# Sixty places in a hand-ordered prologue: an RWKV time-mix kernel with the steps of pairs 4 to 13 moved past their neighbours

## The chip, the core and the metric

The kernel runs on one core of a Trainium2 chip. The core has five engines that work side by side, each with its own queue of instructions: PE (TensorE, matrix products), DVE (VectorE), ACT (ScalarE), POOL (GpSimd) and SP (SyncE, which here only issues transfers). Sixteen DMA engines move data between the chip's main memory and the core's memory. The metric is the device time of one execution in microseconds; lower is better. The kernel before took 287.9 us, the median of three runs (287.43 to 288.99).

## What is computed

For each of 16 batches and 256 channels, a recurrence runs over 2048 time steps. It keeps a weighted sum `aa` of the values v, a sum of weights `bb`, and a running exponent `pp` that keeps the exponentials in range:

```python
for t in range(seq_len):
    kk = k[b, t, :].copy()
    vv = v[b, t, :].copy()
    ww = u + kk
    qq = np.maximum(pp, ww)
    e1 = np.exp(pp - qq)
    e2 = np.exp(ww - qq)
    output[b, t, :] = (e1 * aa + e2 * vv) / (e1 * bb + e2 + 1e-08)
    ww = pp - w + kk
    qq = np.maximum(ww, kk)
    e1 = np.exp(ww - qq)
    e2 = np.exp(kk - qq)
    aa = e1 * aa + e2 * vv
    bb = e1 * bb + e2
    pp = qq
```

k, v and the output are 33.5 MB each in fp32, so 67 MB are read and 33.5 MB written.

## The kernel before

Time is cut into 16 chunks of 128 steps. For one chunk, the 16 batches are handled four at a time; such a quarter of a chunk is called a pair here (pair n = 4 * chunk + quarter, n from 0 to 63), and the four pairs of one chunk are a group. One pair is a tile of 128 time steps by 4 batches by 256 channels, 512 KB of k and 512 KB of v.

The work on a pair is split into named steps, each on one engine. In the order of the data:

- LK n and LV n load k and v. The first three pairs are loaded by SP, the others by POOL, in one queue. k of pairs 3 to 11 is loaded straight into a `kr` buffer (four of them); from pair 12 on it goes into a `kf` buffer (five), and RK n rounds it into `kr`, on DVE or, for one pair in four, on POOL. Pairs 0 to 2 also have an RK. v goes into a `vr` buffer (four).
- R q n and L q n (q = 0 or 1, `rows` and `logs`) are PE's work that builds the exponents of pair n in one of two PSUM buffers, X0 or X1. X q n (`exps`) is ACT's exponential of it into the ring `EZR`, and frees the X buffer and, with q = 1, the PE side of `kr`.
- CV n casts v to bf16 into `vb` (two buffers; DVE for the first ten pairs, POOL after that), TV n (DVE) multiplies, and S n (PE) sums over time into `TOT`.
- Once per group c, after the fourth S: CS c (DVE copies TOT), TU c (PE turns it), SL c (ACT, logarithm), FR c and OF c (DVE), SW c (ACT), CH c and SS c (DVE), TK c (PE turns the states back into `TURN`), BK c (DVE copies TURN to `cb`), and SN c and KP c (DVE, what the next group starts from).
- DEN n and NUM n (PE) form denominator and numerator; DEN uses an X buffer, NUM the buffer `num`. LN n and INV n (ACT) form the inverse, MUL n (DVE) multiplies into `ot`, and ST n (SP) stores it, ten pairs behind the load.

Between PE's steps stand "zeros", products of a zero tile written to `TURN`, whose result nobody uses. `Z`, `Z0` and `ZAT` say how many stand ahead of which kind of step; none are written in the stretch of the plan that lies from a TK to its BK (the flag `quiet`).

The order of everything is set by a planner at the end of the function. Each step has a place, a number; places come from the table `P`, and an entry of `AT` replaces the place of one step by name ("TK 0": 7.205). The planner takes again and again the first step in order of place whose inputs have been planned and whose buffer is free:

```python
todo = sorted(ops, key=lambda x: ops[x]["place"])
while todo:
    for name in todo:
        o = ops[name]
        if all(x not in ops or "done" in ops[x] for x in o["after"]) and (xs if o["take"] == "X" else free.get(o["take"], 1)):
            break
```

An engine runs its steps in just this order, and waits at the head of its queue. Which X buffer an R, L, X or DEN gets follows from the order too: the buffer that was freed first in the plan. A kr slot that a load takes must have been read by the L that used it; the waits for that are worked out from the order as well.

Of the kernel before, what the change touches and what calls it, by code (L numbers as in the profile page):

```python
# [15 lines left out]
def kernel(  # L16
# [46 lines left out]
         "Z": {"DEN": 0, "L": 1, "NUM": 0, "TK": 4, "S": 0, "TU": 1, "R": 0}}  # L63

    AT = {"INV 55": 69.0, "SL 15": 69.1, "LN 56": 69.2, "SW 15": 75.7, "FR 15": 69.3, "TU 0": 5.01, "FR 0": 5.02,
# [4 lines left out]

    ZAT = {"DEN 0": 4, "TU 1": 4, "R 0 11": 4}

# [123 lines left out]
    X = [psx.tile([128, 2, D], F32, tag=f"X{a}", name=f"X{a}") for a in range(2)]  # L196
# [31 lines left out]
    AS, D1, L1, A0, FR, BC, A2 = range(7)  # L228
# [268 lines left out]
```

## Time and profile before

| | before |
|---|---|
| median of three runs | 287.9 us (287.43 to 288.99) |
| profiled execution | 288.48 us, span 286.8 us |
| granted TensorE clock, mean | 0.988 |
| PE busy | 269.5 us (94%) |
| ACT busy | 258.9 us (90%) |
| DVE busy | 248.0 us (86%) |
| POOL busy | 175.9 us (61%) |
| moved by DMA | 101.19 MB, mean 353 GB/s |

The page shows one execution. Busy time counts an engine's instructions and not its waits; PE's matrix products are pipelined, so that a busy PE is not one at its peak. The page's second part cuts the span into 40 slices of 7.2 us with the busy tenths of each engine. The chain that ended last follows the work back from the end, at each step to what released it. A timeline lists instructions with their start, duration, engine, line and buffers, and in brackets the engine's idle time before and what ended it. A step is found in it by its line: L207 is R, L213 is L, L216 is X, L225 is TV, L200 is RK, L220 is CV, L252 is S, L258 is CS, L265 is TU, L309 is TK, L313 is BK, L329 is DEN (into X) or NUM (into num), L341 and L346 are LN and INV, L361 is MUL, L114 and L117 are loads of k, L121 loads of v, L155 the zeros.

### The profile page before, as it was taken

To read this page: it belongs to the slowest core of one execution; us is meant where nothing else is said; L and a number is where in the kernel's file an instruction comes from. 1 tells how busy PE (TensorE), PEld (TensorE's weight loads), DVE (VectorE), ACT (ScalarE), POOL (GpSimd) and SP (SyncE) were. 2 spreads that over 40 slices of the span, in tenths; PEclk is the share of its full clock that TensorE was granted. 3 is DMA by queue.
4 is the path that set the end of the run, shared out by engine and by line. 5 is a ranking of instruction groups with operands and counts; after the bars stand their busy time and mean duration, and the time that the engine had idled before them with its cause. 6 is when DMAs were issued, how large, how long until landed. Compare 5 with 4: busy or idle time off the path is not lost.

```text
span 286.8 us, 7960 instructions
## 1 busy us (share of the span) xinstructions
PE 269.5 (94%) x3215; PEld 135.5 (47%) x3215; DVE 248.0 (86%) x422; ACT 258.9 (90%) x291; POOL 175.9 (61%) x218
## 2 busy tenths in 40 slices
PE   7998999999999999999999999999999999997850
PEld 6444544454445444554545455454545445443430
DVE  5678879899898989899898989999898989799860
ACT  1787679999999999999999999999999999998990
POOL 8364457875757676775757686775757684422330
PEclk9999999999999999999999999999999999999995
DMA  6999999999999999999999999999999999975885
GB/s 222 350 350 345 350 348 333 394 394 390 399 391 387 389 395 387 386 376 393 368 397 385 388 391 386 390 382 391 380 390 367 393 389 387 332 208 141 249 253 167
DMA packets 59052, 101.19 MB, mean 353 GB/s; under 512 B 5152, under 2 KB 44200, under 8 KB 59016
## 3 DMA queue, kind: packets, MB, share of 16 engines
q0 software_dynamic: 21584, 65.42, 65.5%
q1 hardware_dynamic: 37280, 35.14, 36.5%
q8 instruction: 25, 0.41, 0.6%
q10 hardware_dynamic: 152, 0.14, 0.2%
q14 instruction: 11, 0.09, 0.1%
HBM read 67.12 MB, written 33.55 MB: 351 GB/s over the span
## 4 chain that ended last, share of the span: by engine, by line
PE 77%; ACT 8%; DMA 5%; DVE 5%; issue 3%; POOL 1%; DVEq 0%; POOLq 0%; ACTq 0%
PE X L213 19%; PE X L329 15%; PE num L329 12%; PE X L207 11%; PE TURN L155 10%; PE TOT L252 6%; DMA kr<-in_k_dram 3%; ACT rd L341 3%; ACT EZR L216 3%; DVE ot L361 2%; ACT rd L346 2%; PE TOT L265 2%; DMA WUf<-in_u_dram 2%; PE TURN L309 1%; DVE EZR L225 1%
## 5 line engine op out<-in xcount | busy, mean ns | idle before, releaser
L216 ACT ACTIVATE EZR<-X 128x1024 bf16<-128x1024 f32 x128 | 126.9, 1013 | 11.4 <-PE X L213 11.4
L220 POOL CAST vb<-vr 128x1024 bf16<-128x1024 f32 x54 | 56.4, 1045 | 69.6 <-DVE EZR L225 66.8
L225 DVE TENSOR_TENSOR EZR<-EZR,vb 128x2048 bf16<-128x2048 bf16 x64 | 77.9, 1219 | 0.4
L361 DVE TENSOR_TENSOR ot<-num,rd 128x1024 f32<-128x1024 f32 x60 | 73.3, 1221 | 3.9 <-ACT rd L346 3.6
L346 ACT ACTIVATE rd<-rd 128x1024 f32<-128x1024 f32 (+1 forms) x65 | 68.0, 1046 | 2.0
L341 ACT ACTIVATE rd<-X 128x1024 f32<-128x1024 f32 (+1 forms) x65 | 65.8, 1012 | 2.8 <-PE X L329 1.0
L155 PE MATMUL TURN<-Z 128*128 128x192 bf16 x271 | 53.7, 267 | 1.5 <-DVE Z L139 1.4
L207 PE MATMUL X<-WU,CO 64*64 64x512 bf16 x512 | 51.9, 390 | 0.9 <-DVE WU L182 0.5
L121 POOL DMA_DIRECT2D vr<-in_v_dram x61 | 46.2, 757 | 5.0 <-DVE vb L220 5.0
L155 PEld LDWEIGHTS <-Z 128*128 128x128 bf16 x271 | 25.1, 103 | 50.7 <-issue 49.1
L213 PE MATMUL X<-kr,NLE 128*128 128x512 f32 x128 | 45.6, 437 | 0.5 <-DMA kr<-in_k_dram 0.4
L213 PE MATMUL X<-kr,NLZ 128*128 128x512 f32 x128 | 45.4, 436 | 0.0
L114 POOL DMA_DIRECT2D kf<-in_k_dram x52 | 39.6, 762 | 0.0
L200 DVE CAST kr<-kf 128x1024 fp32r<-128x1024 f32 x39 | 32.6, 863 | 3.9 <-DMA kf<-in_k_dram 3.7
L207 PEld LDWEIGHTS <-CO 64*64 64x64 bf16 x512 | 15.8, 105 | 31.5 <-issue 26.3
L329 PE MATMUL X<-EZR,S 64*64 64x512 bf16 x256 | 26.2, 394 | 1.6 <-ACT rd L341 1.0
L329 PE MATMUL X<-cb,Id 64*64 64x512 bf16 x256 | 25.9, 376 | 0.0
L329 PE MATMUL X<-EZR,Id 64*64 64x512 bf16 x256 | 25.8, 376 | 0.0
L329 PE MATMUL num<-EZR,SN 64*64 64x512 bf16 x240 | 24.3, 386 | 1.4 <-DVE ot L361 1.4
L252 PE MATMUL TOT<-EZR,OH 128*32 128x256 bf16 x512 | 23.6, 277 | 0.8 <-DVE EZR L225 0.5
L329 PE MATMUL num<-cb,IdN 64*64 64x512 bf16 x240 | 23.9, 376 | 0.0
L329 PE MATMUL num<-EZR,IdN 64*64 64x512 bf16 x240 | 23.9, 376 | 0.0
(69 smaller groups left out, 269.8 us busy)
## 6 DMA issues: line engine op xcount, KB each, us to landing
vr<-in_v_dram POOLq DMA_DIRECT2D x61, 512.0 KB, 7.8
kf<-in_k_dram POOLq DMA_DIRECT2D x52, 512.0 KB, 8.7
out_dram<-ot SPq DMA_DIRECT2D x64, 256.0 KB, 10.1
out_dram<-ot SPq DMA_DIRECT2D x116, 128.0 KB, 9.8
kr<-in_k_dram POOLq DMA_DIRECT2D x9, 512.0 KB, 9.2
ot<-in_k_dram SPq DMA_DIRECT2D x3, 512.0 KB, 5.1
ot<-in_v_dram SPq DMA_DIRECT2D x3, 512.0 KB, 7.8
out_dram<-ot POOLq DMA_DIRECT2D x11, 128.0 KB, 3.6
```

What stands on the lines that cost most here:

```text
L121: K((SP if n < BYSP else POOL).dma_start(out=vr, in_=rows_of(v, n)))
L155: K(PE.matmul(TURN[:, 0:192], Z[:, 0:128], Z, start=first, stop=True, skip_group_check=True))
L207: K(PE.matmul(X[a][o:o + HS, i, :].rearrange("p (n d) -> p n d", n=2), CO[r:r + HS, q, :], WU[r:r + HS, :].unsqueeze(1).broadcast_to([HS, ...
L213: K(PE.matmul(X[a][:, i, :], (NLE, NLZ)[q], km[:, i, :], start=False, stop=True, skip_group_check=True))
L216: K(SC.activation(ez(n)[:, q, 1], X[a], ACT.Exp))
L220: K((DVE if n < EARLY else POOL).tensor_copy(vb, VR.pop(n)))
L225: K(DVE.tensor_mul(ez(n)[:, :, 0], ez(n)[:, :, 1], vb.unsqueeze(1).broadcast_to([128, 2, 2, D])))
L252: K(PE.matmul(t[32 * j:32 * j + 32, 0:256], OH[:, s:s + 32], ez(n)[:, 0, 1 - q, i, 256 * x:256 * x + 256], start=p == 0 and x == 0, stop=p ...
L329: K(PE.matmul(out_tile[o:o + HS, i, :], left, right, start=s == 0, stop=s == 2, tile_position=(r, o), skip_group_check=True))
L341: K(SC.activation(RD[n][:, i], X[a][:, i], ACT.Ln, scale=RS))
L346: K(SC.activation(RD[n][:, i], RD[n][:, i], ACT.Exp, scale=-1.0))
L361: K(DVE.tensor_mul(o.rearrange("p (i n) d -> p i (n d)", i=2)[:, i], NUM[n][:, i], RD[n][:, i]))
```

## The change

Only the table `AT` changes: sixteen entries that were there get another number, or the same with more digits, and some fifty steps of pairs 4 to 13 and of the groups 0 and 1 get an entry for the first time. The loads, their sizes and the tables for the zeros are as before.

```diff
-          "SW 0": 6.2, "TK 0": 7.205, "CV 7": 6.4, "TV 5": 5.1, "S 4": 5.3, "S 5": 7.195, "TV 6": 6.3,
-          "S 6": 7.21, "S 7": 8.1, "CH 0": 6.32, "SS 0": 6.33, "BK 0": 7.21, "CV 6": 5.2, "TV 7": 7.3,
-          "KP 0": 8.6, "TV 8": 8, "R 0 6": 5.0, "R 0 8": 7.19, "R 0 9": 7.9, "CS 1": 8.2, "TU 1": 8.3,
-          "SN 0": 8.15, "FR 1": 8.95, "CV 9": 8.0, "SW 1": 9.6, "RK 11": 9.1}
+          "SW 0": 6.2, "TK 0": 7.3825, "CV 7": 6.4, "TV 5": 5.04, "S 4": 5.0888, "S 5": 7.195, "TV 6": 5.76,
+          "S 6": 7.21, "S 7": 8.1, "CH 0": 4.9413, "SS 0": 4.9544, "BK 0": 8.6215, "CV 6": 6.08, "TV 7": 7.3,
+          "KP 0": 8.6221, "TV 8": 8.6296, "R 0 6": 5.0494, "R 0 8": 7.19, "R 0 9": 7.9, "CS 1": 8.6308,
+          "TU 1": 9.035, "SN 0": 8.6394, "FR 1": 8.95, "CV 9": 8.6209, "SW 1": 9.6, "RK 11": 9.1, "L 1 8": -2.785,
...
+          "X 1 9": 6.4325, "TV 12": 9.8475, "R 1 6": -0.0325, "CV 5": 4.9675, "R 1 12": 4.1225, "BK 1": 1.4363,
+          "X 0 6": 4.1544, "R 1 13": 4.46, "L 0 11": -0.0437, "X 1 5": 4.1565, "L 1 9": -0.0381}
```

Many of the new places leave a step where it was, since only the order counts. On each engine's queue this is what differs (before, then after; steps not named stay in place):

```
PE    S 3, R 0 6, L 0 6, R 1 6, L 1 6, TU 0, S 4   ->  S 3, TU 0, R 0 6, L 0 6, R 1 6, L 1 6, S 4
      S 5, TK 0, S 6                               ->  S 5, S 6, TK 0
      one zero each ahead of L 0 9 and L 1 9       ->  none
ACT   X 0 5, X 1 5, X 0 6, SL 0, X 1 6             ->  X 1 5, X 0 5, SL 0, X 0 6, X 1 6
      X 0 9, X 1 9                                 ->  X 1 9, X 0 9
DVE   CV 7, BK 0, TV 7, SN 0, CS 1, KP 0           ->  CV 7, TV 7, BK 0, KP 0, CS 1
      CV 8, TV 8, CV 9, FR 1                       ->  CV 8, CV 9, TV 8, SN 0, FR 1
      SN 1, RK 12, TV 9                            ->  SN 1, TV 9, RK 12
POOL  LK 3, LK 4, LV 3, LK 5                       ->  LK 3, LV 3, LK 4, LK 5
      CV 10, LK 14, LV 13                          ->  CV 10, LV 13, LK 14
SP    the same
```

Three things follow from this order. Pairs 6 to 8 use the two X buffers the other way round (R 0 6 gets X1), and so does pair 9, until X 1 9 ahead of X 0 9 turns it back for pair 10. LK 4 is planned after L 1 2 instead of ahead of RK 2, so that RK 2 gets a kr slot that was never used and LK 4 the slot of pair 0, which L 1 0 must have read. And BK 0 is planned after L 1 9 instead of ahead of L 0 9, so that the zeros of those two steps fall into the stretch where none are written.

8 rows, old and new, of the table AT are left out of this document.

## The prediction

> **What bounds the kernel now.** I read the page's forty slices first, then the waits, then the chain that ended last in order of time, and last the timelines of PE, DVE and POOL around pairs 4 to 17.
>
> ```profile
> PE   7998999999999999999999999999999999997850
> ACT  1787679999999999999999999999999999998990
> DMA  6999999999999999999999999999999999975885
> GB/s 222 350 350 345 350 348 333 394 394 390 399 391 387 389 395 387 386 376 393 368 397 385 388 391 386 390 382 391 380 390 367 393 389 387 332 208 141 249 253 167
> ```
>
> A slice is 7.2 us. The DMA engines are full from slice 1 to slice 34, at some 348 GB/s while only loads run and some 390 once stores are mixed in. ACT has gaps in the first six slices; PE is full from slice 4.
>
> ```profile
> 45.53:61.71 16.18, 16.16 (x198) 7.96 (x198) 15.16 (x26) 15.93 (x19) 11.86 (x14) 1.00 1.03 380
> ```
>
> That is one group of four pairs in the steady part, by windows (PE, PEld, DVE, ACT, POOL busy, clock, DMA share, GB/s). PE is busy 16.16 of 16.18 us at full clock. So the steady part runs at PE's pace, and time won or lost ahead of it reaches the end as it is, unless the loads cannot follow.
>
> The chain of waits through the first forty us:
>
> ```profile
> 19.58 9.35 DMA kr<-in_k_dram
> 28.97 0.72 PE X L213 x2
> 30.71 0.33 PE TOT L252 x8
> 31.04 0.77 PE TURN L155 x8
> 31.81 0.24 PE TURN L309 x4
> 32.07 0.70 DVE cb L313
> 32.82 0.24 PE TURN L155
> 33.06 0.50 PE X L213 x2
> 34.97 0.44 DVE ts L258
> 35.45 0.69 PE TOT L265 x4
> 38.53 0.77 PE X L329 x12
> ```
>
> The load of k for pair 8 (k8) lands at 28.93 and releases L 0 8. From there the chain is PE, with two excursions to DVE: BK 0 (the copy of TURN) at 32.07, because the zero ahead of L 0 9 writes TURN and must wait for that copy, and CS 1 at 34.97. At 38.53 DEN 0 opens the steady part.
>
> What DVE and PE do where loads come just in time, in the timeline:
>
> ```profile
> 41.07 0.70 DVE L200 CAST kr<-kf 128x1024 fp32r<-128x1024 f32 x1 [1.77 <-DMA kf<-in_k_dram]
> 41.68 1.22 DVE L225 TENSOR_TENSOR EZR<-EZR,vb 128x2048 bf16<-128x2048 bf16 x1
> 42.82 1.22 DVE L361 TENSOR_TENSOR ot<-num,rd 128x1024 f32<-128x1024 f32 x1
> 53.54 1.25 DVE L200 CAST kr<-kf 128x1024 fp32r<-128x1024 f32 x1
> 54.77 1.23 DVE L361 TENSOR_TENSOR ot<-num,rd 128x1024 f32<-128x1024 f32 x1
> 56.34 0.41 PE L329 MATMUL num<-EZR,SN 64*64 64x512 bf16 x4
> ```
>
> These are RK 12, TV 9 and MUL 0, then RK 16, MUL 3 and PE's NUM 4, which needs the num buffer that MUL 3 frees.
>
> **The change part by part.** Landing times below are issue plus the time to landing that the trace gives for that one issue.
>
> 1. *LK 4 behind LV 3 on POOL's queue, and now behind L 1 0.* Before, k3 and k4 were issued at 5.70 and about 6.4, v3 at 7.24; they landed at 14.10, about 15.5 and 16.94. RK 2 now takes the fourth kr slot and k4 the slot that L 1 0 frees (its chain end is 9.80; the trace shows 0.37 us from there to an issue), so it is issued at 10.2. v3 moves up one place to about 15.5, k4 down to about 17.0. L 0 4 ran at 17.55: 0.5 us of room, cost 0. CV 3 had waited 0.65 us for v3; that goes, but PE's next need of it is S 2, behind R 0 4 to L 1 4 anyway: gain 0. LK 5 to LK 8 still wait for the same L steps, and the set of loads ahead of k8 is the same sixteen, so k8 stays at 28.9. Bounds: if the load needs no longer than the quickest of POOL's shown (6.0 us), it lands at 16.2 by itself and the queue decides; if it takes the longest of the early k loads (9.9 us), it lands at 20.1. I take 17.0, as other loads are still ahead of it in the queue; the rest is a rival.
>
> 2. *TU 0 ahead of R 0 6, and X 1 5 ahead of X 0 5 on ACT.* L 0 6 lost 0.60 us waiting for k6 (22.91), and S 4 lost 0.43 (25.27 to 25.70) waiting for SL 0. TU 0 (0.61) now fills part of the first, and S 4 comes later. ACT stands still until L 1 5 ends (21.58 plus 0.1), so X 1 5 runs to 22.7, X 0 5 to 23.7 (1.02 each), SL 0 to 24.0. PE: R 0 6 waits for X 1 5 and TU 0, so 23.2; L 1 6 ends 25.25, S 4 25.6, L 1 7 27.65 (0.34, 0.19, 0.50 for R, zero and L), against 24.64, 26.04 and 28.08 before. R 0 8 needs X 0 7, done 27.7, and ends 28.05. L 0 8 then waits for k8 as before. Gain 0, cost 0: k8 covers it. If the swap cost 0.9 us more than this, it would come out.
>
> 3. *S 6 ahead of TK 0, BK 0 behind TV 7, and two zeros gone.* The zeros ahead of L 0 9 and L 1 9 fall away because BK 0 is now planned after them. Before, from TK 0's chain end 32.05 to L 0 9 at 33.06 went 1.01 us, with S 6 and R 0 9 inside it. Now S 6 (0.33) and R 0 9 (0.34) stand in the path and the wait for BK 0 does not: 0.67. Gain 0.34. The second zero was 0.19 on the chain; a zero inside a batch of eight costs 0.77/8 = 0.10, one with a wait 0.24. I take 0.19, the row of that zero: total 0.53, bounds 0.34 (nothing from the second) to 0.58. DVE follows: SS 0 ends 30.4, CV 7 31.15 (v7 lands 30.41), TV 7 32.4, BK 0 33.1, KP 0 33.3, all ahead of S 7's end at 34.4. CS 1 then ends 34.9 and TU 1 starts 34.9 instead of 35.45.
>
> 4. *X 1 9 ahead of X 0 9.* ACT idles from 31.8 to L 1 9's end, 34.1; X 1 9 to 35.1, X 0 9 to 36.2. R 0 10 takes X 1 9's buffer at 35.6, R 1 10 the other at 36.65. SL 1 slips behind X 0 9 to 36.5 (36.45 before), and FR 1 now stands behind TV 8 at 38.7. Cost 0; room 0.45 us.
>
> 5. *TV 8 behind CV 9; SN 0 late; TV 9 ahead of RK 12.* CV 9 waits for v9 (36.64), so TV 8 ends 38.55 instead of 37.4; its readers (CV 10 at 40.02, S 8 at 43) do not notice. FR 1, OF 1, SN 1 end at 40.0, ahead of SW 1 (INV 0 ends 40.95). TV 9 fills the 1.77 us in which DVE waited for k12 and ends 41.2, RK 12 41.85, MUL 0 starts there, 1.0 earlier than 42.82; ST 0 leaves 1.0 earlier. MUL 1 is held by INV 1 and is only 0.5 earlier. So PE gains nothing more here.
>
> 6. *LV 13 ahead of LK 14.* CV 10 still starts at 40.02, held by v10, so v13 is issued at 41.0 and k14 at 42.07, and they exchange landings: k14 48.47 instead of 47.0. RK 14 ran at 49.07 and would now run at 48.55: 0.1 us of room. Each tenth later pushes TV 11 and MUL 2, but RK 16 behind them waits for k16 anyway, so up to 0.5 us costs 0.
>
> 7. *What takes part of it back.* k16 lands at 53.49 by queue and bytes; I leave that where it is, since POOL's work from 40.02 to 48.5 is unbroken and is not moved. RK 16 therefore cannot start earlier than 53.5, MUL 3 ends at 56.0 as now, and NUM 4 cannot start before 56.04 instead of 56.34. Of 0.53 us, 0.30 is left. Later groups show the same pattern (RK 20 begins at 69.76, when k20 lands), with similar room.
>
> Sum: 0.53 - 0.23 = 0.30 us gained. The profiled execution took 288.48 (span 286.8), so 288.18; it lies 0.58 above the median of the runs, 287.9, and in that frame the forecast is 287.6. With the ends of point 3 and a full clip (0) or none (0.58) it is 287.3 to 287.9.
>
> **The rivals.**
>
> A. *Nothing is left: the loads set the pace.* For it: DMA shares near or above 1.0 in every steady group, and RK 28 at 102.78 after a wait of 0.80 for its load. Against: PE's 16.16 of 16.18. Time 287.9.
>
> B. *The loads come earlier.* From k6 to k12 they land 1.4 to 1.7 us apart, but v4 came 3.06 after k5 (18.50 to 21.56), though DMA moved 340 to 350 GB/s throughout: part of a later load was served ahead. If the new order of v3 and k4 avoids that, everything behind lands 1.5 earlier. L 0 8 then starts at 28.25, when R 0 8 and its zero end: 0.7 gained, plus 0.53, and k16 no longer clips: 1.2, so 286.7. The Trainium skill, "DMA: Bandwidth & Descriptors", section on queues, rings and completion order, says that a DMA's sixteen engines finish independently, so completion need not follow issue; by that rule the place in the queue does not fix k8's landing and B or its opposite is open. The trace shows landings in issue order but unevenly spaced, which does not decide it.
>
> C. *Slower: k4 late.* It is issued 3.8 us later than before. If it takes 9.9 us it lands at 20.1, 3.1 behind its place, and k5 to k8 queue behind it: k8 at 32.0, 3.06 lost less 0.53: 287.9 + 2.5 = 290.4. It decides once k4 lands after 17.5, and costs more than 0.5% once the queue slips by 2 us. Against: queue and bytes ahead of it last until about 15.5, five us after its issue.
>
> D. *The edit does not change the order.* Excluded: in the built program PE, ACT, DVE and POOL each have places exchanged, as in the points above.
>
> **How the numbers follow.** Chances: main case 0.50, A 0.16, B 0.18, C 0.16. Half a per cent, 1.44 us, is about what a measurement of this kernel can tell from no change. Main and A lie inside. B at 286.7 is just inside at its price, and beyond it (under 286.46) if the steady part also loses a stall such as the 0.38 us that NUM 16 waited at 105.47, behind RK 28, or the spread of runs adds to it: two thirds of B and 0.06 from the main case's tail make faster 0.18. C at its price is slower, at half of it within: two thirds of it, and 0.04 for a miscounted ACT wait in points 2 and 4, make slower 0.15. Same: 0.67. The range takes in B and the smaller half of C: 286.3 to 289.1.
>
> **What would show it.** L 0 8 still released by its load near 28.9; k4 landing near 17.0 and no wait at L 0 4; no DVE step between TK 0 and L 0 9 in the chain; TU 1 near 34.9 and DEN 0 near 38.0; RK 12 after TV 9 with a wait under 0.1; MUL 0 near 41.85; RK 16 waiting some 0.4 us for k16; steady groups of 16.18. Wrong if k4 or k8 lands a slot earlier or later, if R 0 6 or R 0 10 waits for ACT longer than computed, or if RK 14 waits over 0.5 us.

## The result and the profile after

The changed kernel takes 289.12 us, the median of 20 runs (287.61 to 291.45), against 288.1 us of the kernel before (20 runs, 287.12 to 289.09). The ratio is 1.0035, 95% interval 1.0018 to 1.0052: 1.0 us slower, where 0.3 us faster was forecast. The times also scatter more: their standard deviation is 0.95 us against 0.63.

The profiled execution took 288.52 us (span 286.8, mean clock 0.993), so it is one of the quick ones, and by its span there is no difference from before at all (also 286.8). What follows from it shows where the steps went; that the kernel is slower as a rule shows only in the run times and in the experiments.

The page's slices of the changed kernel, 7.2 us each:

```profile
PE   7989999999999999999999999999999999997860
ACT  1767689999999999999999999999999999998990
DMA  7999999999999999999999999999999999964895
GB/s 222 351 350 345 350 347 339 393 394 389 394 391 387 391 392 385 389 369 396 386 390 381 391 393 386 392 378 394 354 395 385 385 390 385 357 187 136 248 265 164
```

and its second steady group, by windows (PE, PEld, DVE, ACT, POOL busy, clock, DMA share, GB/s):

```profile
45.53:61.71 16.18, 16.17 (x199) 7.87 (x197) 14.63 (x25) 15.85 (x19) 11.75 (x15) 1.00 1.04 377
```

The steady part is as before, PE busy 16.17 of 16.18 us. Of PE's first slices the third, 14.3 to 21.5 us, has fallen from 9 to 8 and the fourth has risen from 8 to 9: PE lost time around 17 us and had it back soon after.

The chain that ended last, from X 0 7 (ACT, at 27.58) to DEN 0:

```profile
27.58 0.98 ACT EZR L226
28.56 0.04 issue
28.60 0.41 PE X L217 x4
...
29.20 0.61 PE X L223 x2
...
31.38 0.77 PE TURN L165 x8
32.15 0.22 PE TURN L319 x4
32.37 0.34 PE X L217 x4
32.71 0.66 PE X L223 x2
33.37 0.34 PE X L217 x4
33.71 0.66 PE X L223 x2
...
34.75 0.44 DVE ts L268
...
35.23 0.69 PE TOT L275 x4
35.92 0.34 PE X L217 x4
36.26 0.19 PE TURN L165
36.45 0.49 PE X L223 x2
...
38.31 0.77 PE X L339 x12
```

Lines are ten higher than before (L223 is L, L217 R, L319 TK, L275 TU, L339 DEN and NUM, L235 TV, L230 CV, L210 RK, L371 MUL). Three things are to be seen. L 0 8 is no longer released by its load: it runs behind ACT, R 0 8 and a zero, at 29.20 in the chain and 29.08 in the timeline, and k8 had landed at 29.01. The excursion to DVE between TK 0 and L 0 9 is gone. And L 0 9 and L 1 9, which now run without a zero ahead of them, take 0.66 us each on the chain, where L 0 10 at 36.45, behind its zero, takes 0.49.

The timeline of DVE, POOL and PE in the changed kernel, at the three places that matter:

```profile
15.79 0.69 DVE L230 CAST vb<-ot 128x1024 bf16<-128x1024 f32 x1 [0.85 <-DMA ot<-in_v_dram]
17.67 0.40 PE L262 MATMUL TOT<-EZR,OH 128*32 128x256 bf16 x6 [0.88 <-DVE EZR L235]
...
40.00 1.05 POOL L230 CAST vb<-vr 128x1024 bf16<-128x1024 f32 x1 [3.18 <-DVE U L290]
40.07 2.06 DVE L235 TENSOR_TENSOR EZR<-EZR,vb 128x2048 bf16<-128x2048 bf16 x1
42.05 0.96 DVE L210 CAST kr<-kf 128x1024 fp32r<-128x1024 f32 x1
42.94 1.20 DVE L371 TENSOR_TENSOR ot<-num,rd 128x1024 f32<-128x1024 f32 x1
...
53.83 0.75 DVE L210 CAST kr<-kf 128x1024 fp32r<-128x1024 f32 x1 [0.57 <-DMA kf<-in_k_dram]
```

First, CV 2 waits 0.85 us for v2, and S 1 waits 0.88 for TV 1, which stands behind CV 2 on DVE; neither waited before (CV 2 ran at 14.67 there). Second, TV 9, put into the 1.77 us in which DVE had been idle, takes 2.06 us instead of 1.22, and in those same 1.77 us POOL runs CV 10. Before, CV 10 ran there alone:

```profile
40.02 1.04 POOL L220 CAST vb<-vr 128x1024 bf16<-128x1024 f32 x1 [2.87 <-DMA vr<-in_v_dram]
```

MUL 0 thus starts at 42.94, 0.12 later than before, not 1.0 earlier. Third, RK 16 waits for k16, as forecast.

### The profile page after: what moved, and what is told of

The parts are those of the page before. It is cut to its first block, busy times and chain, and to the rows that moved or that the text cites. A ratio compares the mean times of both kernels' runs of the same rounds, so it can differ in the third digit from the quotient of the medians.

```text
span 286.8 us, 7960 instructions
## 1 busy us (share of the span) xinstructions
PE 269.4 (94%) x3213; PEld 135.1 (47%) x3213; DVE 248.0 (86%) x422; ACT 258.7 (90%) x291; POOL 173.8 (61%) x218
## 4 chain that ended last, share of the span: by engine, by line
PE 76%; ACT 9%; DVE 5%; DMA 4%; issue 2%; SPq 1%; DVEq 0%; ACTq 0%
PE X L223 19%; PE X L339 15%; PE num L339 12%; PE X L217 11%; PE TURN L165 10%; PE TOT L262 6%; DMA ot<-in_v_dram 4%; ACT rd L351 4%; ACT EZR L226 3%; DVE ot L371 3%; ACT rd L356 2%; PE TOT L275 2%; DVE EZR L235 1%; PE TURN L319 1%; SPq L124 1%
## 5 line engine op out<-in xcount | busy, mean ns | idle before, releaser
L230 POOL CAST vb<-vr 128x1024 bf16<-128x1024 f32 x54 | 56.3, 1043 | 70.9 <-DVE EZR L235 67.8
L235 DVE TENSOR_TENSOR EZR<-EZR,vb 128x2048 bf16<-128x2048 bf16 x64 | 78.8, 1232 | 0.4
L371 DVE TENSOR_TENSOR ot<-num,rd 128x1024 f32<-128x1024 f32 x60 | 73.2, 1220 | 4.2 <-ACT rd L356 3.9
L217 PE MATMUL X<-WU,CO 64*64 64x512 bf16 x512 | 51.9, 390 | 0.6 <-DVE WU L192 0.2
L223 PE MATMUL X<-kr,NLE 128*128 128x512 f32 x128 | 45.6, 438 | 0.0
L223 PE MATMUL X<-kr,NLZ 128*128 128x512 f32 x128 | 45.5, 437 | 0.0
L210 DVE CAST kr<-kf 128x1024 fp32r<-128x1024 f32 x39 | 31.7, 842 | 3.9 <-DMA kf<-in_k_dram 3.8
L217 PEld LDWEIGHTS <-CO 64*64 64x64 bf16 x512 | 15.8, 105 | 30.8 <-issue 25.5
L339 PE MATMUL X<-EZR,S 64*64 64x512 bf16 x256 | 26.2, 395 | 1.6 <-ACT rd L351 1.0
L339 PE MATMUL num<-EZR,SN 64*64 64x512 bf16 x240 | 24.3, 387 | 1.8 <-DVE ot L371 1.8
L339 PE MATMUL X<-cb,Id 64*64 64x512 bf16 x256 | 25.8, 376 | 0.0
L339 PE MATMUL X<-EZR,Id 64*64 64x512 bf16 x256 | 25.8, 376 | 0.0
L339 PE MATMUL num<-cb,IdN 64*64 64x512 bf16 x240 | 23.9, 376 | 0.0
L339 PE MATMUL num<-EZR,IdN 64*64 64x512 bf16 x240 | 23.9, 376 | 0.0
```

The costliest lines, as they stand in the source:

```text
L217: K(PE.matmul(X[a][o:o + HS, i, :].rearrange("p (n d) -> p n d", n=2), CO[r:r + HS, q, :], WU[r:r + HS, :].unsqueeze(1).broadcast_to([HS, ...
L223: K(PE.matmul(X[a][:, i, :], (NLE, NLZ)[q], km[:, i, :], start=False, stop=True, skip_group_check=True))
L230: K((DVE if n < EARLY else POOL).tensor_copy(vb, VR.pop(n)))
L235: K(DVE.tensor_mul(ez(n)[:, :, 0], ez(n)[:, :, 1], vb.unsqueeze(1).broadcast_to([128, 2, 2, D])))
L339: K(PE.matmul(out_tile[o:o + HS, i, :], left, right, start=s == 0, stop=s == 2, tile_position=(r, o), skip_group_check=True))
L371: K(DVE.tensor_mul(o.rearrange("p (i n) d -> p i (n d)", i=2)[:, i], NUM[n][:, i], RD[n][:, i]))
```

## The experiments

Each kernel is the one before or the changed one with a few entries of `AT` put back or put in; a removed entry is marked with a minus. The ratio is always to the kernel before, timed on the same chip. TK 1 is the start of that step in the profile; before it is 47.23, in the changed kernel 47.14. In some of these kernels a line number is one higher than in the changed one.

**The two moves on POOL's queue, each alone and each undone**

Before, with LV 3 ahead of LK 4 and nothing else:

```diff
+ "LK 4": 1.6125
```

> The kernel before with one thing of the change: LV 3 ahead of LK 4 on POOL, with k4 in the slot that L 1 0 frees. Theory H (the early loads cost the time: v3 and k3 compete with v2 on SP's queue and k4 comes late): ratio to before 1.002 to 1.005, the wait of DVE for v2 near 0.8 us and of S 1 for TV 1 near 0.9 us as in the profile after. Theory T (the swap of v13 and k14 costs it) and theory P (PE and DVE order, which brings the steady part ahead of its loads): 0.999 to 1.001, though the wait of S 1 may show.

Measured: 288.89 us, ratio 1.0017 (0.9999 to 1.0036). This lies between the two expectations. The wait of CV 2 for v2 is there (0.86 us). TK 1 is at 47.26: by then the profiled execution has lost nothing.

What the late v2 shared the DMA engines with is in the trace's DMA records. v2 is the last load on SP's queue, in packets of 1024 bytes. Before, k4, also in packets of 1024 bytes, was next on POOL's queue when v2 was under way; now it is v3, in packets of 4096. GB/s of each queue, in steps of half a microsecond, with a third kernel that has k4 next, as before (that with DVE's moves alone, further below):

```
us             12.5  13.0  13.5  14.0  14.5  15.0
before  POOL    221   324   383
        SP      129    41     0
after   POOL    199   338   311   311   293   356
        SP      166    76    45    25    31     0
DVE's   POOL    164   213   317   338   373   344
moves   SP      176   137    57    29    16     4
```

SP's queue runs dry at 13.6 us before, at 15.0 after and at 15.3 in the third. The Trainium skill, "DMA: Bandwidth & Descriptors", section on queues, rings and completion order, says that each DMA engine goes round the queues it has work for packet by packet. By that, if the profile's packets are what it means, an estimate gives four fifths to the queue whose packets are four times as large. The trace of the changed kernel is near that at first, 338 against 76 (82%), and then shows more, 311 against 45 and 25 (87 and 93%). But the third kernel comes to as much, 317 against 57 and 338 against 29 (85 and 92%), with packets of 1024 bytes on both queues, and its DVE waits for v2 too:

```profile
15.81 0.69 DVE L220 CAST vb<-ot 128x1024 bf16<-128x1024 f32 x1 [0.67 <-DMA ot<-in_v_dram]
```

So the size of the packets is not shown to be the cause. Over the 20 profiles of this document, v2 landed between 14.1 and 16.7 us in the twelve kernels with LV 3 ahead of LK 4, 15.5 on average, and between 13.9 and 15.7 in the other eight, 14.8 on average. Three of the twelve have it at 14.1 to 14.4, as the kernel before (14.11). The move thus goes with a later v2 by some 0.7 us on average, but one profile does not settle it, and what decides it within an execution stays open.

The changed kernel without this move, then the other move alone, and the changed kernel without that one:

```diff
- "LK 4": 1.6125
```

> The changed kernel with LK 4 back ahead of LV 3. Theory H: ratio to before 0.997 to 1.000, since only the gain of the other parts is left. Theories T and P: 1.002 to 1.005 as for the whole change. In all three: no wait of S 1 for TV 1, and L 0 8 again released by its load near 28.9.

```diff
+ "LV 13": 9.3
```

> The kernel before with one thing of the change: LV 13 ahead of LK 14 on POOL. Theory T: ratio to before 1.002 to 1.005, RK 14 waiting for k14 and RK 16 and the later roundings of k20, k24 ... waiting more than before (1.9 us in four waits). Theories H and P: 0.999 to 1.001, waits as before.

```diff
- "LV 13": 8.9975
```

> The changed kernel with LK 14 back ahead of LV 13. Theory T: ratio to before 0.997 to 1.000. Theories H and P: 1.002 to 1.005, with waits of DVE for k16, k20 ... near the 3.8 us in seven waits of the whole change.

Measured: 288.56 (ratio 1.0008, 0.9994 to 1.0023), 288.42 (1.0000, 0.9983 to 1.0016) and 288.49 (1.0011, 0.9990 to 1.0031). LV 13 ahead of LK 14 costs nothing by itself that its measurement can tell. With either move undone the loss is smaller, but the profiles of the two show something that neither move explains. The timeline of the kernel without the first move, around CV 10, and RK 13 with RK 14:

```profile
39.75 1.22 DVE L236 TENSOR_TENSOR EZR<-EZR,vb 128x2048 bf16<-128x2048 bf16 x1
39.81 2.05 POOL L231 CAST vb<-vr 128x1024 bf16<-128x1024 f32 x1 [3.26 <-DVE U L293]
40.88 1.53 DVE L211 CAST kr<-kf 128x1024 fp32r<-128x1024 f32 x1
...
48.14 1.05 POOL L231 CAST vb<-vr 128x1024 bf16<-128x1024 f32 x1
48.34 2.02 DVE L211 CAST kr<-kf 128x1024 fp32r<-128x1024 f32 x2
```

Here it is POOL that loses the meeting with TV 9: CV 10 takes 2.05 us, and all of POOL's queue behind it is late. CV 12, two casts on, then meets RK 13 and RK 14 on DVE, which take 2.02 us together where they took 1.32 before. What that leads to is in the chain of the same kernel:

```profile
48.42 1.35 DVE kr L211
...
49.81 0.72 PE X L224 x2
...
51.94 0.80 PE X L340 x12
...
52.76 1.03 ACT rd L352
...
53.82 1.06 ACT rd L357
54.88 0.62 ACT EZR L227
...
63.97 0.84 PE X L340 x12
```

L 0 13 waits for RK 13, and from 52.8 to 64 us the chain is ACT's, LN, INV and X one behind the other, before PE takes over again. The group from TK 1 to TK 2, by windows, in this kernel and in the changed kernel's profile:

```profile
46.74:63.52 16.78, 16.43 (x200) 7.98 (x198) 16.14 (x25) 16.02 (x19) 12.94 (x16) 1.00 1.04 388
```

```profile
47.14:63.24 16.10, 16.09 (x199) 7.86 (x198) 14.55 (x25) 15.77 (x19) 11.67 (x15) 1.00 1.04 391
```

16.78 us instead of 16.10, DVE busy 16.14 instead of 14.55 with the same 25 instructions, ACT at 16.02. So the meeting at 40 us has several outcomes, and one costs a whole group 0.6 us.

**Both moves undone, and the changed kernel again; half of the stores left out**

```diff
- "LK 4": 1.6125
- "LV 13": 8.9975
```

> The changed kernel with both swaps of loads undone, so the order of PE, ACT and DVE alone. Theory P: ratio to before 1.001 to 1.004, with TK 1 some 0.4 us earlier than before and one or two more waits of PE behind late loads. Theory H: 0.997 to 1.000.

> The changed kernel beside the others on one chip, so that they can be compared with it. Both theories: ratio to before 1.002 to 1.005.

For the question whether full DMA engines take the gain back, half of the stores of the first 52 pairs were left out, of before and of after:

```diff
-        for h in range(1 if shared(n) else 2):
+        for h in range((1 if shared(n) else 2) if n >= BYPOOL else 0):
```

> The kernel before without the two 128 KB stores of each of pairs 0 to 51 (half of their output is not written), so that the DMA engines have 13.6 MB less to move once the steady part begins. Theory P (the DMA engines are full in the steady part, loads of k arrive too late at random, each costing PE some 0.37 us): no wait of DVE for k after pair 16, no wait of PE for MUL ahead of 250 us, time 0.3 to 1.5 us under the kernel before, and less spread. Rival (the waits for k have nothing to do with the stores): same waits, same time.

> The changed kernel without the same stores. Theory P: what the order of PE and DVE gains by pair 10 (0.22 us at DEN 0 in its profile) now stays to the end, so 0.1 to 0.4 us faster than the kernel before without these stores; the loss of the change appears only with full DMA engines. Theory H (the order of the early loads costs the time, before any store): 0.5 to 1.0 us slower than the kernel before without these stores, as with them.

Measured: both undone 289.16 (1.0025, 1.0001 to 1.0050); the changed kernel again 289.31 (1.0042, 1.0017 to 1.0067), which shows its loss again; with half the stores, before 287.74 (0.9984, 0.9966 to 1.0003) and after 289.0 (1.0019, 1.0001 to 1.0038). With both moves on POOL's queue undone the median still lies 0.9 us above before, though the interval nearly reaches 1; so the two moves are not the whole of the loss, and most of it seems to lie elsewhere. With half the stores the profiles show no wait of RK for a load behind pair 16 any more, and the change is as much slower as with all of them: that full DMA engines are the cause falls.

In the changed kernel's second profile DVE loses the meeting ahead of TV 9. SN 1, a copy of 128x64 that takes 0.21 us in the first profile, starts 0.05 us behind CV 10, takes 1.05 and ends when CV 10 is done; TV 9 then runs in its usual time. With both moves undone it is the step ahead of SN 1, the last of OF 1, that takes 1.04 instead of 0.19 (its DVE line, last, with CV 10 at 39.73):

```profile
39.91 1.04 POOL L230 CAST vb<-vr 128x1024 bf16<-128x1024 f32 x1 [2.95 <-DVE U L290]
39.96 1.05 DVE L295 COPY U<-U 128x64 f32<-128x64 f32 x1
40.92 1.21 DVE L235 TENSOR_TENSOR EZR<-EZR,vb 128x2048 bf16<-128x2048 bf16 x1
...
39.77 1.04 DVE L292 TENSOR_SCALAR U<-U 128x64 f32<-128x64 f32 x1
```

These small steps stood at 38.2 to 39.3 before. In the changed kernel they come to 39.1 to 40.2, since TV 8 now stands between CV 9, which waits for v9, and them. So TV 8's place has a part in the meeting as well as RK 12's.

**DVE's order: undone, alone, and the gain of TK 0 alone**

The new theory was that TV 9 ahead of RK 12 is the cause. The changed kernel with RK 12 back ahead of TV 9, and the same with TV 8 back ahead of CV 9 as well:

```diff
- "RK 12": 10.93
+ "RK 12": 9.4
```

> The changed kernel with RK 12 back ahead of TV 9 on DVE. Theory C (TV 9 now starts at 40.0, in the same tenth of a microsecond as POOL's CV 10; one of the two waits for the other, a cast of 2.05 instead of 1.05 us where POOL loses, and then CV 12 meets RK 13 and 14 and L 0 13 waits): DVE idles for k12 again, CV 10 takes 1.05, RK 13 and 14 together 1.3, no wait of L 0 13, spread as before (standard deviation 0.7 instead of 1.0), ratio to before 1.000 to 1.002. Theory H alone (the early loads): as the whole change, 1.003 to 1.004.

```diff
- "RK 12": 10.93, "TV 8": 8.6296
+ "RK 12": 9.4,   "TV 8": 8.6206
```

> The changed kernel with RK 12 back ahead of TV 9 and TV 8 back ahead of CV 9. Theory C: as with RK 12 alone undone, 1.000 to 1.002. If TV 8 behind the wait for v9 costs something itself, up to 0.001 less than that kernel.

Before with both of these moves alone, and before with point 3 of the prediction alone:

```diff
- "TV 8": 8
+ "TV 8": 8.05, "RK 12": 10.93
```

> The kernel before with TV 8 behind CV 9 and TV 9 ahead of RK 12, nothing else. Theory C: TV 9 and CV 10 meet near 40.0, one of them takes about 1 us longer than by itself, the spread grows, ratio to before 1.000 to 1.003. Theory H: 0.999 to 1.001, and RK 12 without a wait.

```diff
- "TK 0": 7.205,  "BK 0": 7.21, "TV 7": 7.3,  "S 6": 7.21
+ "TK 0": 7.3825, "BK 0": 8.01, "TV 7": 7.35, "S 6": 7.36
```

> The kernel before with S 6 ahead of TK 0, TV 7 ahead of BK 0 and the two zeros gone, nothing else. From the forecast's third point: TU 1 and TK 1 0.4 to 0.5 us earlier than before (46.8 instead of 47.23), and if nothing meets on DVE and POOL, ratio to before 0.998 to 0.9995.

Measured: RK 12 back 288.68 (1.0008, 0.9984 to 1.0032); RK 12 and TV 8 back 288.2 (0.9986, 0.9968 to 1.0004); DVE's moves alone 288.67 (0.9999, 0.9980 to 1.0019); point 3 alone 288.3 (0.9995, 0.9977 to 1.0012), with TK 1 at 47.09. With both of DVE's moves undone the loss is gone, and the ratio lies a little under the 1.000 to 1.002 that was expected; putting them alone into the kernel before does not bring the loss. With RK 12 alone put back the interval takes in both answers; the scatter was expected to fall to 0.7 us, and did not: the standard deviation is 1.1. v2 was late in the kernel with both put back (S 1 waits 1.00 us for TV 1) and on time in that with RK 12 alone, so the late v2 by itself need not make a kernel slow. In the kernel before with DVE's moves alone, TV 9 comes 0.5 us ahead of CV 10, and the two overlap only in part:

```profile
39.36 1.22 DVE L225 TENSOR_TENSOR EZR<-EZR,vb 128x2048 bf16<-128x2048 bf16 x1
39.84 1.64 POOL L220 CAST vb<-vr 128x1024 bf16<-128x1024 f32 x1 [2.49 <-DMA vr<-in_v_dram]
40.89 1.14 DVE L200 CAST kr<-kf 128x1024 fp32r<-128x1024 f32 x1 [0.30 <-DMA kf<-in_k_dram]
```

CV 10 takes 1.64 us, 0.6 more than alone, POOL is that much late instead of 1.0, and the group behind TK 1 takes 16.15 us. So the order of the two steps is not enough by itself. That it takes their starting in the same tenth of a microsecond, which only the rest of the change brings about, fits these profiles, but no run sets that moment alone.

**Once more with half the stores, and PE's and ACT's moves alone**

The changed kernel with half the stores again, then the same with RK 12 back, and with RK 12 and TV 8 back (edits as above):

> The changed kernel without the two 128 KB stores of each of pairs 0 to 51 (that half of their output is not written), beside the two that follow on one chip. It was 1.0 us over the kernel before with the same stores left out. Theory C: again 1.0 us over that, so 288.5 to 289.1 us, with the meeting of TV 9 and CV 10 in its profile.

> The same (stores left out as before), with RK 12 back ahead of TV 9. Theory C: 0.5 to 1.0 us under the changed kernel without these stores, CV 10 of 1.05 us, and 16.1 us from TK 1 to TK 2. If the loss lies elsewhere (TV 8 behind CV 9, or the early loads): the same time as that.

> The same (stores left out as before), with RK 12 back ahead of TV 9 and TV 8 ahead of CV 9. Theory C: as with RK 12 alone undone, within 0.2 us. If TV 8 behind the wait for v9 is the cause: 0.5 to 1.0 us under both others.

The moves of TV 8 and TV 9 and both on POOL's queue undone, so that those on PE and ACT and the rest of DVE's are left:

```diff
- "LK 4": 1.6125, "LV 13": 8.9975, "RK 12": 10.93, "TV 8": 8.6296
+ "RK 12": 9.4, "TV 8": 8.6206
```

> The changed kernel with both swaps of loads, RK 12 and TV 8 undone, all outputs written: what is left is the order of PE and ACT and of BK 0, KP 0 and SN 0. Theory C: 0.997 to 0.9995 of before, TK 1 0.4 us earlier, no meeting of TV 9 and CV 10. If the order of PE and ACT is the cause: 1.002 to 1.004.

Measured: 288.34 (1.0012, 0.9987 to 1.0037), a little less than the 288.5 to 289.1 that was expected, 287.65 (0.9985, 0.9969 to 1.0001), 287.77 (0.9993, 0.9972 to 1.0015); and 288.33 (0.9992, 0.9971 to 1.0014) for what is left on PE and ACT. With RK 12 back, POOL runs CV 10 in its 1.04 us while DVE waits for k12, as in the kernel before (timeline of the second):

```profile
40.00 1.04 POOL L231 CAST vb<-vr 128x1024 bf16<-128x1024 f32 x1 [3.31 <-DVE U L293]
41.04 0.69 DVE L211 CAST kr<-kf 128x1024 fp32r<-128x1024 f32 x1 [1.03 <-DMA kf<-in_k_dram]
```

The last kernel keeps point 3 and the exchanges on ACT, has TK 1 at 46.93 and loses nothing; what it gains, if anything, is less than its measurement can tell.

**The late v2 without its consequence, and both suspected causes gone**

```diff
+ "TV 1": 1.1
```

> The changed kernel with TV 1 one place forward on DVE, ahead of CV 2; nothing else. v2 still arrives late (SP's queue gets 25 to 76 GB/s from 13.0 us on) and CV 2 still waits about 0.85 us for it, but TV 1 no longer stands behind CV 2. If what the late v2 costs goes by way of TV 1 and S 1: S 1 waits under 0.3 us instead of 0.88, L 0 8 starts at 29.0, released by k8, TK 1 is 0 to 0.2 earlier than in the changed kernel (47.14), and the ratio is 0.1 to 0.2% under that of the change: 1.0020 to 1.0030, since TV 9 and CV 10 still meet at 40 us. If the late v2 costs nothing (its loss is taken up before TK 1 in any case): 1.0035, as the change.

```diff
- "RK 12": 10.93
+ "RK 12": 9.4, "TV 1": 1.1
```

> The changed kernel with both suspected causes taken out and the rest kept: TV 1 ahead of CV 2, and RK 12 back ahead of TV 9 (so that CV 10 on POOL again runs while DVE waits for k12). If these two are the whole of the loss: ratio 0.998 to 1.000, TK 1 near 46.9, CV 10 1.04 us, RK 13 and 14 at their times of before. If some of the loss lies elsewhere in the new order: 1.001 or above.

Measured: 288.93 (1.0021, 1.0000 to 1.0042) and 288.36 (1.0012, 0.9993 to 1.0030). With TV 1 ahead of CV 2, S 1 waits no more and L 0 8 is held by k8 again (timeline of the first kernel):

```profile
14.47 1.17 DVE L236 TENSOR_TENSOR EZR<-EZR,vb 128x2048 bf16<-128x2048 bf16 x1
15.81 0.69 DVE L231 CAST vb<-ot 128x1024 bf16<-128x1024 f32 x1 [0.17 <-DMA ot<-in_v_dram]
...
29.06 0.74 PE L224 MATMUL X<-kr,NLE 128*128 128x512 f32 x2 [0.57 <-DMA kr<-in_k_dram]
```

That is 0.14% under the first measurement of the change, well inside the intervals; TK 1 comes at 47.01. In this profile POOL loses the meeting again (CV 10 takes 2.06 us), and the group behind TK 1 takes 16.85 us. The second kernel has TK 1 at 46.88 and that group at 16.10, as expected, but lies a little over the 0.998 to 1.000 that was set for it; its interval takes in both answers.

**What the runs say together.** Of the eight profiled kernels with TV 9 ahead of RK 12 in the changed kernel's surroundings, five show POOL losing (CV 10 at 1.97 to 2.08 us), with 16.43 to 16.85 us from TK 1 to TK 2, mean 16.70. The other three have 16.10 to 16.16, and the kernel before 16.16. In all eight, what starts first keeps its time: TV 9 where it is 0.04 to 0.15 us ahead of CV 10; CV 10 where it is there first, and then the DVE step that starts 0.04 to 0.07 us behind it is held, TV 9 itself in one profile and a small step ahead of it in two.

The mean times say the same: the six of these kernels that store everything lie 0.26 to 1.00 us above before on their chips, 0.64 on average; the four with RK 12 back lie between 0.31 below and 0.22 above, -0.05 on average. With half the stores the two groups of two are at +0.23 and -0.52. That is some 0.7 us by both comparisons, with a standard error of about 0.2 by the spread of the runs. It is not the worth of RK 12's place alone, since three of the six kernels with RK 12 back have TV 8 back too. The two that store everything and have RK 12 alone put back lie 0.17 and 0.22 above before, 0.44 under the six, with a standard error of about 0.25; the one with half the stores lies 0.60 below.

The start of TK 2 adds up what comes ahead of it: 63.58 on average in the eight (63.22 to 64.05), 63.10 in the six with RK 12 back (62.95 to 63.38), 63.39 in the kernel before. So the traces show about 0.5 us between the two orders, but against the kernel before only 0.2, and the changed kernel's own two profiles are 0.1 ahead of it there (63.24 and 63.30). From TK 2 to TK 13 every kernel, of either order, runs groups of some 16.2 us, with one to four of 16.53 to 16.64 among them where all stores are made and none where half are left out, and it takes 18.5 to 19.9 us from TK 15 to the end. The longest execution that was profiled, 289.6 us with RK 12 and TV 8 put back, has three such groups and an end of 19.90; the shortest that stores everything, 287.23 with PE's and ACT's moves alone, has one and 18.69. Single executions differ there by up to 2 us, and no run ties that to the order of the first steps.

## Why the prediction was wrong

The step that failed is point 5, "TV 9 fills the 1.77 us in which DVE waited for k12". Those 1.77 us were idle on DVE, but POOL was running CV 10 in them, and the trace of before showed that: 40.02 to 41.06 in POOL's timeline. I took the gap as free because no instruction of DVE's stood in it, and priced TV 9 at its usual 1.22. Side by side the two engines do not run at their usual speed: TV 9 takes 2.06, or SN 1 ahead of it takes 1.05 and TV 9 starts at 40.92, or CV 10 takes 2.05. The Trainium skill, "GPSIMD Engine Reference", section on specifications, states that POOL shares its SBUF interfaces with DVE, with contention where DVE's instruction has two SBUF inputs, as TV's has, or runs in a 2-port perf mode. The trace agrees, and gives the price: the loser is late by 0.8 to 1.0 us. Whether SN 1's copy, with one input, ran in such a mode no run here shows. None of the forecast's rivals had this. Point 7 leaned on the same assumption, that "POOL's work from 40.02 to 48.5 is unbroken and is not moved": in five of eight profiles it is moved by about 0.8 us (CV 12 at 48.14 and 48.47 in two of them, 47.36 with TV 1 ahead of CV 2 and RK 12 back), and RK 13 and RK 14 take longer: the group behind TK 1 has 16.43 to 16.85 us where the forecast had 16.18. That takes back 0.25 to 0.67 us, of a gain that the forecast put at 0.30.

Point 1 failed in what it looked at. For the loads it named it was right: LK 4 was issued at 9.78 (10.2 forecast) and landed at 16.98 (17.0), k8 at 29.01 (28.9), and rival C, k4 late, did not happen. But SP's queue, which still runs beside it, was left out, and with it v2, whose cast is one place in the DVE order ahead of TV 1. In the changed kernel's profile v2 landed 1.6 us later than before (15.70 against 14.11), and through CV 2, TV 1 and S 1 it moved R 0 8's end from the forecast 28.05 to 29.01, so that all of the cover that k8 gave was used up. By TK 1 it costs little: 0.03 us in the profile of this move alone, and 0.13 in the changed kernel (47.14, against 47.01 with TV 1 ahead of CV 2).

Point 3 had the mechanism right and a size wrong. The wait for BK 0 and both zeros went, and L 0 9 starts at 32.71 instead of 33.06, the 0.34 worked out. That the figures meet is luck: S 5 and S 6 behind each other take 0.55 on the chain, so that S 6 added 0.22 and not 0.33, and L 0 8, held by R 0 8, ended 0.12 later than before and took that back. But an L without a zero ahead of it takes 0.66 on the chain instead of 0.49, so that L 0 9 gives 0.17 back, and the second zero gone is worth 0.19 less 0.17, not 0.19. TU 1 came at 35.23 (34.9 forecast, 35.45 before) and DEN 0 at 38.31 (38.0, and 38.53 before): 0.22 gained up to there instead of 0.53.

Points 2, 4 and 6 came out as worked out, if the shift by S 1's wait is allowed for: k14 landed at 48.55 (48.47 forecast), RK 14 was not held by it, and RK 16 waited 0.57 us for k16 (some 0.4 forecast). Rivals A and B are answered too: with half the stores the loads hold nothing, and the change is still the slower one; and nothing behind k4 landed 1.5 us earlier.

What stays open is the size. The meeting is shown, and so is the longer group behind it in five of eight profiles, 0.56 us longer, some 0.35 on average. That it makes the changed kernel 1.0 us slower is not shown: the traces have 0.2 us of that by TK 2. The slowest executions of the change, 289.5 us and more (seven of its 20, none of before's 20 beside them), were not caught in a trace: the two profiled ones took 288.52 and 288.42. How much of the loss goes by the late v2 is not settled either. LV 3 ahead of LK 4 alone has 1.0017, but with an interval that reaches to 0.9999, and no delay at TK 1 to show for it. And whether TV 8's place has a share of its own in the time is open: with it and RK 12 put back the ratios are 0.9986 and 0.9992, with RK 12 alone 1.0008 and 1.0012, and the intervals overlap.

No kernel tried beats the one before by more than its measurement can tell.

## What to carry to other kernels

A gap on one engine is free only if nothing on the other engines uses it: before a step is moved into an idle stretch of DVE, read POOL's timeline for that stretch, and ask which of the two will lose. When two queues share the DMA engines, a new order on one may change how fast the other drains, so look at the last load of every queue that is still running, not only at the loads that moved. And a gain of a few tenths in the first 40 us can be seen in one profile while the median goes the other way; look at the scatter of the runs, and at the profiles of several variants, before believing it.

## What the runs showed of the hardware that was not expected

- A POOL cast of 128x1024 from fp32 to bf16 and a DVE multiply of 128x2048 in bf16 that start within 0.15 us of each other cost one of them about the time of the other: 1.05 became 2.05, or 1.22 became 2.06. The later one loses, by however little: the multiply with starts at 40.00 (POOL) and 40.07 (DVE), the cast with 39.81 and 39.75. So a shift of a tenth decides which queue is late.
- A small DVE step loses in the same way: a copy of 128x64 in fp32, otherwise 0.21 us, took 1.05 when it started 0.05 us behind the same cast, and a DVE step with a scalar operand 1.04 instead of 0.19.
- Over the last 1.5 to 2 us of its last load SP's queue, in packets of 1024 bytes, got under 80 GB/s of some 320 to 415, beside a queue with packets of 4096 bytes (changed kernel) and, from 13.5 us on, beside one with packets of 1024 (DVE's moves alone).
- A matrix product in fp32 behind R's 64x64 products takes 0.66 us on the chain, and 0.49 if one product of 128x128 zeros, itself 0.19, stands between: the zero costs almost nothing.
